# A hybrid recurrent decoder step on one core: loads moved to another DMA queue, two products made one, a sum taken from DMA to VectorE, and a new cut of the closing LayerNorm

## The chip, the cores and the metric

The kernel runs on one core of a Trainium2 chip. The metric is device time of one execution in microseconds; of the kernel before there are three runs, and their median counts. Engines are named as in the profile: PE is TensorE (PEld its weight loads), DVE is VectorE, ACT is ScalarE, POOL is GpSimd, SP is SyncE, which here only issues DMAs.

## The reference

One inference step of a single layer: a prompt of 512 tokens and 8 samples of one token each, which bring their states along. Everything is fp32.

```python
hq, hf, hi, hz, rq, rk, rv, rz, mq, mk, mv, mz, mo, mi, mf, gates = split(x @ w_in)   # 2048 -> 19464 columns
o_a = hgrn2(silu(hq), 1 - f, hi, f)           # 8 heads, 128 x 128;  f = lb + (1 - lb) * sigmoid(hf)
o_b = retention(rotary(rq), rotary(rk), rv)   # 4 heads, 256 x 256
h_c = mlstm(mq, mk, mv, mi, mf) * sigmoid(mo) # 4 heads, 256 x 256, with n and m beside C
ys  = head_norm(o) * silu(z)                  # for each of the three
out = sum_n(sigmoid(gates_n) * (ys_n @ w_branch[n])) @ w_out
y   = layernorm(alpha * x + out) * ln_g + ln_b
```

For a sample of retention, one step is `S = gamma * S + k v^T`, `o = q^T S`; for mLSTM the same with factors of its own, and a normaliser n.

## The kernel before

Tokens lie along the free axis: 512 of the prompt and 8 of the samples, `N` = 520 columns, in two halves of `HN` = 260. Each fp32 operand of a large product is cut into a high part, rounded to fp32r (`hi`, by ACT), and the rest (`lo`, by DVE); a product is then hi x hi, hi x lo and lo x hi on PE, in `PD` banks of PSUM.

The projection goes over 76 units of 256 columns of `w_in`. The first three are done plainly (`classical_w`). The other 73 use a Winograd form of Strassen's scheme (`strassen_unit`): seven items of 24 matmuls instead of eight, each on one block or sum of blocks of the weights. The blocks b11, b12 lie in one weight tile, b21, b22 in the next; tiles `R` come from a ring of three, 1 MB each. One of the sums, b11 + b12, lies in a tile of its own, `TT`. DVE makes it where the unit's columns are deinterleaved (`deint`) or where there is no unit before it; for the other units SP loads b11 into TT and an accumulating DMA of Pool's queue adds b12. The order of the units is: 16 for HGRN2, 16 for retention, 20 for mLSTM, 24 for the merge gates. Then come the branch products (`bunit`, 24 units of 256 columns of `w_branch`), the output projection (`ofin`), and LayerNorm.

`dense` writes out the items one after the other and yields after every few matmuls; at each yield `side_step` may add a step of three queues of side work: preparation, the scans of the heads (`a_head`, `b_head`, `c_head`), and the samples (`a_samp`, `bc_samp`). Whether it does is settled when the program is built, by a planner (`Clock`): it prices each instruction (in `Counted`), keeps a time for each engine and for DMA, and lets a step in when its time is due and DVE and ACT aren't further ahead than `clk.next` plus a margin. On the chip each engine just runs its instructions in the order written. A step whose data the planner holds for late (`late`) is put off.

Projected rows are stored to DRAM by Pool (`parked`, to `pk_...`) and loaded again by the head that needs them (`ld`) into slots `SL` of a pool of 16. `bc_samp(h, br)` handles the eight samples of one head in pairs: SP loads each state (`lds_`, 256 KB), Pool loads v (`ldv`), ACT scales v by the two halves of k into `tm` and `vb`, DVE updates the state's two halves, Pool stores it, and PE forms `o` by two products per sample, one for each half, whose weights are the query masked by sample (`qmask`, tile `qmt`: column b holds q of sample b, the others zeros); all go into the same PSUM rows `po` (`os` in the profile).

`norm_rows(c0)` normalises two blocks of 128 tokens: ACT scales a piece by the row's factor, DVE multiplies by `ln_g` (`lng`), DVE or Pool adds `ln_b` (`lnb`), SP stores. Blocks 0 and 1 come while PE works on the last half of the output, blocks 2 and 3 and the samples (`norm_samples`) after its end (`finish`).

Nearly all instructions are issued in the wrapper of `Counted`, line 165, and DMAs in its lines 142 and 143; so rows are told apart by the tiles that they write and read.

Of the kernel before, what the change touches and what calls it, by code (L numbers as in the profile page):

```python
# [17 lines left out]
D = 2048  # L18
# [100 lines left out]
class Counted:  # L119
# [3 lines left out]
    def __getattr__(self, op):  # L123
# [22 lines left out]
        def g(*a, **kw):  # L146
# [5 lines left out]
            if me == "pe":  # L152
                if op == "transpose":
                    t = 0.109 if out.shape[-1] > 64 else 0.06
                else:
                    n = a[2].shape[-1]
                    t = max(0.06, 0.00046 * n) if a[2].dtype == F32R else max(0.06, 0.00085 * n)
# [16 lines left out]
def tile_hybrid_step(  # L174
# [153 lines left out]
    qmt = const.tile([128, 2, 8, 8], F32, name="qmt")  # L328
# [97 lines left out]

    class Item:

        def __init__(self, src, mm, post=None, keep=None, nosplit=False):
# [3 lines left out]
            self.late = False  # L433
            self.part = None
# [65 lines left out]
    def strassen_unit(col, deint, fin):  # L500

        src = w_in[0][:, col:col + 256]
# [81 lines left out]
        if prev and not deint:  # L584
# [69 lines left out]
    def classical_rows(src, rws, xf, fin, pre=None):  # L654

        kt = 8 * rws
# [70 lines left out]
    def dense():  # L727
# [5 lines left out]
        for i, it in enumerate(items):  # L733
            it.run("first")
            clk.next = clk.pe + 2.87
# [46 lines left out]
    def ld(nm, k, pre=False):  # L782
        s = sl()
        SY.dma_start(out=v3(s[:, 0:S], 2), in_=d2(ptile(f"{nm}{k}"))[:, :, 0:256], pre=pre)
# [23 lines left out]
    def qmask(q, e):  # L808

        t = qmt[:, e]  # L810
        V.tensor_tensor(out=t, in0=e8, in1=q.unsqueeze(2).to_broadcast([128, NS, 8]), op=MUL)
        return t
# [208 lines left out]
    def a_samp(h):  # L1021
        q, K, f, z = sm("Aq", h), sm("AK", h), sm("Af", h), sm("Az", h)
        hb = {}
        qm = qmask(q, 0)
# [136 lines left out]
    def b_head(h):  # L1161
# [4 lines left out]
        for i in range(2):  # L1166
            SY.dma_start(out=cs2[i][:, 0:S], in_=rope[i, :, 0:S])
# [76 lines left out]
    def bc_samp(h, br):  # L1244
# [18 lines left out]
        def lds_(b):  # L1263
            st = yield from ssl()
            SY.dma_start(out=v3(st[:, 0:512], 2), in_=state_in[0, b, h].rearrange("(p t) v -> p t v", t=2), pre=True)
# [20 lines left out]
        qm = [qmask(q[e], e) for e in range(2)]  # L1286
        po = po1()
        for b0 in range(0, NS, 2):
# [6 lines left out]
            for bs in ([b0, b0 + 1],) if b0 + 1 in lds else ([b0], [b0 + 1]):  # L1295
# [24 lines left out]
                fr(tm)  # L1320
                yield 1
                for b in bs:
                    st = lds.pop(b)
                    for e in range(2):
                        T.matmul(po[0:NS, 0:256], qm[e][:, b, :], st[:, e * 256:(e + 1) * 256],
                                 start=(b == 0 and e == 0), stop=(b == 7 and e == 1))
                    fr(st)
                yield 1
# [249 lines left out]
    def w_unit(col, deint, fin):  # L1578
        strassen_unit(col, deint, fin)

# [36 lines left out]
    for i, (col, deint, fin) in enumerate(wl):  # L1617
# [4 lines left out]
        else:  # L1622
            strassen_unit(col, deint, fin)
# [143 lines left out]
    def norm_rows(c0):  # L1767
# [9 lines left out]
        for c in range(2):  # L1777
            hh = H[:, c0 + c, :]
            for q0, q1, e in (((0, 672, G), (672, 1344, G), (1344, 2048, V)) if c0 + c < 3 else
                              ((0, 640, G), (640, 1152, G), (1152, 1600, V), (1600, 2048, V))):  # L1780
# [326 lines left out]
```

## Time and profile before

| | |
|---|---|
| median of three runs | 2374.71 us (2374.15 to 2378.41) |
| the profiled execution: its time, its span | 2384.39 us, 2382.5 us |
| instructions in the span | 45461 |
| granted TensorE clock, mean | 0.992 |
| moved by DMA | 449.26 MB, 189 GB/s on average |
| on the queue of SP (hardware), of Pool (software) | 312.77 MB, 133.38 MB |

The time in the first row is what is forecast; all rows of the profile belong to the one profiled execution. Busy time is the time in which an engine worked on an instruction; matmuls are pipelined, so the mean of one is longer than the distance of two, and busy times of groups that overlap don't add up. A matmul of fp32 by fp32 leaves two records, one of fp32r leaves one. In the chain of waits each line has its start, its length, and the engine and tile or the DMA that it spent it on.

### The profile page before, as it was taken

The numbers are of one execution on the slowest core, as the hardware profiler recorded it, in microseconds if no ns is written. First come the engines' busy times: TensorE is split into PE (matmuls) and PEld (weight loads), VectorE is DVE, ScalarE is ACT, GpSimd is POOL, SyncE is SP. The second block draws the span as 40 slices with busy tenths as digits, with TensorE's granted clock in tenths as the row PEclk, the third lists the DMA queues.
The fourth block names the chain that finished last, engine by engine and source line by source line (L and its number), as shares of the span: only waits on it lengthen the run. The fifth ranks groups of instructions, "written<-read, shape, count | busy, mean of one in ns | idle before, by whom it ended". The sixth has DMA issues, their size and how long they took to land.

```text
span 2382.5 us, 45461 instructions
## 1 busy us (share of the span) xinstructions
PE 2318.9 (97%) x18677; PEld 2240.8 (94%) x18677; DVE 1603.2 (67%) x2571; ACT 1031.3 (43%) x1611; POOL 490.8 (21%) x653
## 2 busy tenths in 40 slices
PE   7999999999999999999999999999999999999995
PEld 7999999999999999999999899898999999999994
DVE  5777777787778868677777666767676534553336
ACT  4344445445545444454445545554554422222222
POOL 2022221323222132222122222212221100002002
PEclk9999999999999999999999999999999999999997
DMA  6367765647566576767767988889796767755221
GB/s 178 116 158 186 196 161 170 184 151 219 149 204 167 182 213 189 223 216 205 234 184 207 187 246 203 221 200 241 169 252 173 225 201 256 253 192 199 89 72 72
DMA packets 404690, 449.26 MB, mean 189 GB/s; under 512 B 16993, under 2 KB 356865, under 8 KB 402945
## 3 DMA queue, kind: packets, MB, share of 16 engines
q1 hardware_dynamic: 313664, 312.77, 42.3%
q0 software_dynamic: 90384, 133.38, 24.2%
q8 instruction: 147, 2.41, 0.4%
q14 instruction: 63, 0.51, 0.1%
q10 hardware_dynamic: 432, 0.20, 0.0%
HBM read 362.98 MB, written 83.28 MB: 187 GB/s over the span
## 4 chain that ended last, share of the span: by engine, by line
PE 61%; DMA 3%; DVE 1%; ACT 1%; issue 0%; POOL 0%; SPq 0%; DVEq 0%; POOLq 0%; ACTq 0%
PE PD L165 54%; PE s L165 4%; PE os L165 3%; DMA R<-in_w_in_dram 1%; DVE SL L165 1%; DMA out_dram<-SL 0%; DMA R<-in_w_branch_dram 0%; DMA TT<-in_w_in_dram 0%; ACT hi L165 0%; DVE lo L165 0%; ACT SL L165 0%; ACT TT L165 0%; DVE sdd L165 0%; DVE R L165 0%; DVE fmv L165 0%
## 5 line engine op out<-in xcount | busy, mean ns | idle before, releaser
L165 PE MATMUL PD<-XZ,hi 128*128 128x260 f32 x9920 | 1430.0, 285 | 13.3 <-ACT hi L165 10.0
L165 PEld LDWEIGHTS PD<-XZ,hi 128*128 128x128 f32 x9920 | 1282.7, 189 | 30.8 <-ACT hi L165 12.0
L165 DVE TENSOR_TENSOR lo<-R,hi 128x1024 fp32r<-128x1024 f32 (+1 forms) x540 | 646.1, 1198 | 381.2 <-ACT hi L165 161.6
L165 PE MATMUL PD<-XZ,lo 128*128 128x260 f32 x4944 | 799.4, 284 | 0.2 <-DVE lo L165 0.2
L165 ACT ACTIVATE hi<-R 128x1024 fp32r<-128x1024 f32 (+1 forms) x541 | 558.1, 1051 | 499.4 <-PE PD L165 254.8
L165 PEld LDWEIGHTS PD<-XZ,lo 128*128 128x128 f32 x4944 | 679.9, 189 | 5.5 <-issue 4.3
L165 ACT ACTIVATE SL<-PD 128x260 f32<-128x260 f32 x304 | 115.2, 381 | 424.3 <-PE PD L165 363.9
L165 POOL COPY smp<-SL 128x8 f32<-128x8 f32 x104 | 93.1, 895 | 535.3 <-ACT SL L165 344.2
L165 DVE TENSOR_TENSOR R<-R,R 128x1024 f32<-128x1024 f32 x146 | 178.0, 1219 | 6.4 <-DMA R<-in_w_in_dram 6.2
L165 DVE TENSOR_TENSOR SL<-SL 128x256 f32<-128x256 f32 (+9 forms) x315 | 146.4, 501 | 32.9 <-PE s L165 26.5
L165 PE MATMUL PD<-X,hi 128*128 128x260 f32 x1168 | 165.1, 287 | 0.3 <-ACT hi L165 0.3
L165 DVE TENSOR_TENSOR SL<-PD,SL 128x260 f32<-128x260 f32 x219 | 93.0, 425 | 99.4 <-PE PD L165 89.8
L165 PEld LDWEIGHTS PD<-X,hi 128*128 128x128 f32 x1168 | 148.4, 188 | 5.0 <-issue 4.1
L165 PE MATMUL s<-SL 128*128 128x64 f32 (+5 forms) x912 | 147.3, 298 | 0.0
L143 POOL DMA_DIRECT2D TT<-in_w_in_dram x56 | 90.2, 1610 | 272.7 <-DMA TT<-in_w_in_dram 245.5
L165 PEld LDWEIGHTS s<-SL 128*128 128x128 f32 (+1 forms) x912 | 125.0, 187 | 6.2
L165 ACT ACTIVATE SL<-SL 128x520 f32<-128x520 f32 (+5 forms) x156 | 85.2, 565 | 66.4 <-DVE SL L165 64.9
L142 POOL DMA_DIRECT2D out_dram<-SL x100 | 61.0, 614 | 217.9 <-DVE SL L165 196.3
L165 POOL TENSOR_TENSOR rstd<-rva,half 128x4 f32<-128x4 f32 (+3 forms) x35 | 45.2, 1292 | 247.5 <-DVE rva L165 247.4
L165 DVE TENSOR_TENSOR lo<-TT,hi 128x1024 fp32r<-128x1024 f32 x73 | 88.8, 1217 | 3.1 <-ACT hi L165 3.0
L165 DVE TENSOR_TENSOR R<-R 128x1024 f32<-128x1024 f32 x73 | 88.9, 1217 | 0.0
L165 PE MATMUL PD<-X,lo 128*128 128x260 f32 x584 | 84.7, 285 | 0.0
(213 smaller groups left out, 1416.7 us busy)
## 6 DMA issues: line engine op xcount, KB each, us to landing
R<-in_w_in_dram SPq DMA_DIRECT2D x150, 1024.0 KB, 6.3
TT<-in_w_in_dram SPq DMA_DIRECT2D x56, 512.0 KB, 6.4
TT<-in_w_in_dram POOLq DMA_DIRECT2D x56, 512.0 KB, 6.5
R<-in_w_branch_dram SPq DMA_DIRECT2D x24, 1024.0 KB, 6.5
out_dram<-SL POOLq DMA_DIRECT2D x88, 256.0 KB, 5.5
R<-in_w_out_dram SPq DMA_DIRECT2D x16, 1024.0 KB, 5.4
pk_g<-SL POOLq DMA_DIRECT2D x48, 260.0 KB, 4.7
SL<-pk_g SPq DMA_DIRECT2D x48, 260.0 KB, 5.9
```

The source lines that it names most:

```text
L142: return f(out=out, in_=in_)
L143: return f(out=out, in_=in_, accum_op=accum_op)
L165: return f(*a, **kw)
```

## The change

It has six parts.

1. `ld`, the rotary tables of `b_head` and the states of `bc_samp` are loaded on Pool's queue and no longer on SP's.
2. In `bc_samp` the two halves of a state are joined ahead of the product: ACT scales half 0 by the query, DVE adds half 1 times the query, and PE makes one product per sample with the constant mask `e8`. `qmask` remains for HGRN2 alone.
3. In `norm_rows` all additions are on DVE; there are eight equal pieces of 512 columns for each pair of blocks, and ACT scales a piece ahead.
4. For the last 24 units, the gates, `TT` is summed by DVE from the loaded tiles, as for a deinterleaved unit.
5. The planner prices a matmul of fp32 operands at twice as much.
6. The planner's look-ahead is 5.74 us for items of 48 matmuls and 2.87 us for items of 24, in place of 2.87 for all.

```diff
-                    t = max(0.06, 0.00046 * n) if a[2].dtype == F32R else max(0.06, 0.00085 * n)
+                    t = max(0.06, 0.00046 * n) if a[2].dtype == F32R else 2 * max(0.06, 0.00085 * n)
...
+    span = [5.74]
...
+            self.span = span[0]
...
-    def strassen_unit(col, deint, fin):
+    def strassen_unit(col, deint, fin, by_dma=True):
+        span[0] = 2.87
...
-        if prev and not deint:
+        if prev and not deint and by_dma:
...
     def classical_rows(src, rws, xf, fin, pre=None):
+        span[0] = 5.74
...
-            clk.next = clk.pe + 2.87
+            clk.next = clk.pe + it.span
...
     def ld(nm, k, pre=False):
-        SY.dma_start(out=v3(s[:, 0:S], 2), in_=d2(ptile(f"{nm}{k}"))[:, :, 0:256], pre=pre)
+        G.dma_start(out=v3(s[:, 0:S], 2), in_=d2(ptile(f"{nm}{k}"))[:, :, 0:256], pre=pre)
...
-            SY.dma_start(out=cs2[i][:, 0:S], in_=rope[i, :, 0:S])
+            G.dma_start(out=cs2[i][:, 0:S], in_=rope[i, :, 0:S])
...
         def lds_(b):
-            SY.dma_start(out=v3(st[:, 0:512], 2), in_=state_in[0, b, h].rearrange("(p t) v -> p t v", t=2), pre=True)
+            G.dma_start(out=v3(st[:, 0:512], 2), in_=state_in[0, b, h].rearrange("(p t) v -> p t v", t=2), pre=True)
...
-        qm = [qmask(q[e], e) for e in range(2)]
...
-                fr(tm)
                 yield 1
                 for b in bs:
-                    st = lds.pop(b)
-                    for e in range(2):
-                        T.matmul(po[0:NS, 0:256], qm[e][:, b, :], st[:, e * 256:(e + 1) * 256],
-                                 start=(b == 0 and e == 0), stop=(b == 7 and e == 1))
+                    i = (b % 2) * 256
+                    act(out=tm[:, i:i + 256], in_=lds[b][:, 0:256], func=AF.Copy, scale=q[0][:, b:b + 1])
+                yield 1
+                for b in bs:
+                    i, st = (b % 2) * 256, lds.pop(b)
+                    V.scalar_tensor_tensor(out=tm[:, i:i + 256], in0=st[:, 256:512], scalar=q[1][:, b:b + 1],
+                                           in1=tm[:, i:i + 256], op0=MUL, op1=ADD)
                     fr(st)
+                yield 1
+                for b in bs:
+                    i = (b % 2) * 256
+                    T.matmul(po[0:NS, 0:256], e8[:, b, :], tm[:, i:i + 256], start=(b == 0), stop=(b == 7))
+                fr(tm)
...
-            strassen_unit(col, deint, fin)
+            strassen_unit(col, deint, fin, i < len(wl) - 24)
...
-            for q0, q1, e in (((0, 672, G), (672, 1344, G), (1344, 2048, V)) if c0 + c < 3 else
-                              ((0, 640, G), (640, 1152, G), (1152, 1600, V), (1600, 2048, V))):
...
+        pieces = [(c, slice(q0, q0 + 512)) for c in range(2) for q0 in range(0, D, 512)]
...
+        scaled(*pieces[0])
+        for i, (c, qq) in enumerate(pieces):
+            if i + 1 < len(pieces):
+                scaled(*pieces[i + 1])
+            hh = H[:, c0 + c, qq]
+            V.tensor_tensor(out=hh, in0=hh, in1=g[:, qq], op=MUL)
+            V.tensor_tensor(out=hh, in0=hh, in1=b[:, qq], op=ADD)
+            SY.dma_start(out=y_p[0, (c0 + c) * 128:(c0 + c + 1) * 128, qq], in_=hh)
+            clk.latest = 0.0
+            yield 1
```

What this does to the order of instructions, at three places. First PE in the gates' stage, beside the samples of an mLSTM head, before. The products of the projection (`PD`) read `XZ` or `X` and a weight part; `os<-SL,qmt` are the samples' products, `s<-ident` transposes of a head.

```order
L165 MATMUL PD_127<-X_85,hi_121 128x260 x3
L165 MATMUL os<-SL,qmt 8x256 x4
L165 MATMUL PD_127<-X_85,hi_121 128x260 x13
L165 MATMUL PD_127<-X_85,lo_124 128x260 x8
L165 MATMUL PD_128<-XZ,hi_122 128x260 x3
```

The same in the changed kernel; `e_91` is the tile `e8`.

```order
L165 MATMUL s<-ident,SL 128x128 x4
L165 MATMUL PD_125<-XZ,hi_121 128x260 x3
L165 MATMUL os<-SL,e_91 8x256 x2
L165 MATMUL PD_125<-XZ,hi_121 128x260 x4
L165 MATMUL PD_125<-XZ,lo_124 128x260 x8
```

A pair of samples takes two products in place of four. In the whole program PE changes between fp32 products and the projection 656 times, both directions counted, where it was 642.

Second, SP's queue in the gates' stage, before. `R` are the ring of weights, `SL<-in_state_mlstm_c` the samples' states, `SL<-pk_...` loads by `ld`.

```order
L142 DMA SL<-in_state_mlstm_c_dram 128x512 x3
L142 DMA R_118<-in_w_in_dram 128x8x256
L142 DMA R_116<-in_w_in_dram 128x8x256
L142 DMA TT<-in_w_in_dram 128x8x128
L142 DMA R_117<-in_w_in_dram 128x8x256
L142 DMA SL<-in_state_mlstm_c_dram 128x512
L142 DMA R_118<-in_w_in_dram 128x8x256
L142 DMA TT<-in_w_in_dram 128x8x128
L142 DMA SL<-pk_mv_11769 128x2x256
```

SP's queue now, the last loads of the gates:

```order
L142 DMA R_118<-in_w_in_dram 128x8x256
L142 DMA R_116<-in_w_in_dram 128x8x256
L142 DMA R_117<-in_w_in_dram 128x8x256
L142 DMA R_118<-y_106 128x2048
L142 DMA R_116<-in_w_branch_dram 128x8x256
```

Only weights are left on it, one after the other, up to the first load of the branches (`y`). The other loads stand on Pool's queue, here at a place of the same stage, among the stores of gates (`pk_g`), of states (`out`), and the power for a norm (`rstd`):

```order
L142 DMA SL<-pk_mz_13703 128x2x256
L142 DMA out_dram<-SL 128x512
L142 DMA pk_g_10_17267<-SL 128x520
L142 DMA SL<-in_state_mlstm_c_dram 128x512
L142 DMA SL<-vs_111 128x512
L142 DMA SL<-in_state_mlstm_c_dram 128x512 x2
L142 DMA out_dram<-SL 128x512
L142 DMA pk_g_11_17388<-SL 128x520
L165 TENSOR_TENSOR rstd<-rva,half 128x4
```

Pool has 802 instructions where it had 658, SP 353 where it had 550.

Third, DVE at the end, from the last output tile to the norm of blocks 2 and 3: `SL<-SL,lng` multiplies, `SL<-SL,lnb` adds.

```order
-L165 TENSOR_TENSOR SL<-SL,lng 128x704
-L165 TENSOR_TENSOR SL<-SL,lnb 128x704
-L165 TENSOR_TENSOR SL<-SL,lng 128x672 x2
-L165 TENSOR_TENSOR SL<-SL,lng 128x704
-L165 TENSOR_TENSOR SL<-SL,lnb 128x704
+L165 TENSOR_TENSOR SL<-SL,lng 128x512
+L165 TENSOR_TENSOR SL<-SL,lnb 128x512
```

Where a multiplication and an addition alternated with multiplications whose additions Pool made, each multiplication is now followed by its addition; the two new rows are the first of five such pairs.

More of the change, by code (lines that the diff above doesn't have):

```diff
@@ L327, in tile_hybrid_step @@
     e8 = const.tile([128, 8, 8], F32, name="e8")
-    qmt = const.tile([128, 2, 8, 8], F32, name="qmt")
+    qmt = const.tile([128, 8, 8], F32, name="qmt")
     ones = const.tile([128, 1], F32, name="ones")
@@ L806, in put_ys, with qmask @@
         V.scalar_tensor_tensor(out=ysm[:, 8 * br + k, :], in0=psum, scalar=gains[:, br, k:k + 1], in1=z, op0=MUL, op1=MUL)
[L808 to L812, printed above, removed]
+    def qmask(q):
+        V.tensor_tensor(out=qmt, in0=e8, in1=q.unsqueeze(2).to_broadcast([128, NS, 8]), op=MUL)
+        return qmt
     def samp_silu(i0, n):
@@ L1023, in a_samp @@
         hb = {}
-        qm = qmask(q, 0)
+        qm = qmask(q)
         def get(b0):
@@ L1575, in c_head @@
         yield from room(0)
-    def w_unit(col, deint, fin):
-        strassen_unit(col, deint, fin)
     def plain(nm, k0):
@@ L1622, in tile_hybrid_step @@
         else:
-            strassen_unit(col, deint, fin)
+            strassen_unit(col, deint, fin, i < len(wl) - 24)
     first_strassen = 4 * NCL
@@ L1776, in norm_rows, with scaled @@
         yield 1
-        for c in range(2):
-            hh = H[:, c0 + c, :]
-            for q0, q1, e in (((0, 672, G), (672, 1344, G), (1344, 2048, V)) if c0 + c < 3 else
-                              ((0, 640, G), (640, 1152, G), (1152, 1600, V), (1600, 2048, V))):
-                qq = slice(q0, q1)
-                act(out=hh[:, qq], in_=hh[:, qq], func=AF.Identity, scale=r[:, c:c + 1], bias=nm[:, c:c + 1])
-                V.tensor_tensor(out=hh[:, qq], in0=hh[:, qq], in1=g[:, qq], op=MUL)
-                e.tensor_tensor(out=hh[:, qq], in0=hh[:, qq], in1=b[:, qq], op=ADD)
-                SY.dma_start(out=y_p[0, (c0 + c) * 128:(c0 + c + 1) * 128, qq], in_=hh[:, qq])
-                yield 2
+        pieces = [(c, slice(q0, q0 + 512)) for c in range(2) for q0 in range(0, D, 512)]
+        def scaled(c, qq):
+            hh = H[:, c0 + c, qq]
+            act(out=hh, in_=hh, func=AF.Identity, scale=r[:, c:c + 1], bias=nm[:, c:c + 1])
+        scaled(*pieces[0])
+        for i, (c, qq) in enumerate(pieces):
+            if i + 1 < len(pieces):
+                scaled(*pieces[i + 1])
+            hh = H[:, c0 + c, qq]
+            V.tensor_tensor(out=hh, in0=hh, in1=g[:, qq], op=MUL)
[3 more added lines that the diff above has]
+            yield 1
     def norm_samples():
```

## Prediction

> **What bounds the kernel now.** I read the busy shares first, then the same by stage, then the chain of work that ended last, then the waits of the engines that TensorE depends on. The busy shares (busy us, share of the span, instructions):
>
> ```profile
> PE 2318.9 (97%) x18677; PEld 2240.8 (94%) x18677; DVE 1603.2 (67%) x2571; ACT 1031.3 (43%) x1611; POOL 490.8 (21%) x653
> ```
>
> TensorE (PE) has work for 97% of the span, so time falls if PE has less to do or waits less, and hardly otherwise. The stages, with busy us of each engine, granted clock, DMA share and GB/s: 120 to 840 us are the HGRN2 projections, 840 to 1320 the retention heads beside the mLSTM projections, 1320 to 1800 the gates' projections beside the mLSTM heads, then branches, output projection, and the tail.
>
> ```profile
> 120.00:420.00 300.00, 296.86 (x2480) 295.38 (x2479) 230.25 (x344) 140.12 (x218) 69.45 (x82) 1.00 0.66 173
> 420.00:840.00 420.00, 417.16 (x3447) 405.74 (x3446) 331.79 (x571) 202.89 (x349) 117.65 (x153) 1.00 0.62 181
> 840.00:1320.00 480.00, 480.00 (x3752) 453.88 (x3751) 348.90 (x516) 230.32 (x344) 120.91 (x164) 1.00 0.72 206
> 1320.00:1800.00 480.00, 468.96 (x3606) 438.02 (x3606) 333.41 (x571) 245.64 (x386) 107.95 (x140) 0.99 0.88 215
> 1800.00:2180.00 380.00, 377.44 (x3149) 376.43 (x3148) 196.79 (x275) 115.85 (x142) 38.19 (x67) 1.00 0.67 220
> 2180.00:2340.00 160.00, 157.38 (x1300) 155.27 (x1298) 54.81 (x108) 35.38 (x53) 1.47 (x3) 1.00 0.27 86
> 2340.00:2382.50 42.50, 13.84 (x108) 13.25 (x107) 29.36 (x48) 11.82 (x16) 16.91 (x11) 0.68 0.26 101
> ```
>
> PE's idle time between 120 and 2340 us is 3.1 + 2.8 + 0 + 11.0 + 2.6 + 2.6 = 22.2 us. Half of it, 11.0, is in the gates' stage, where DMA is busiest (0.88); 28.7 more is the tail, in which PE has nearly done and DVE works. The clock is granted in full wherever PE is fed, so there is nothing to win there.
>
> **Samples' halves joined.** Of the chain, start and length of three pieces (records of TensorE), and the group of the samples' products:
>
> ```profile
> 1520.98 1.82 PE os L165 x8
> 1522.81 3.08 PE PD L165 x24
> ...
> 1886.12 289.55 PE PD L165 x2421
> ```
>
> ```profile
> L165 PE MATMUL os<-SL,qmt 128*8 128x256 f32 x256 | 61.9, 380 | 0.0
> ```
>
> For each sample and head of retention and mLSTM, PE multiplied two state halves with a masked query: 8 x 8 x 2 = 128 matmuls, which leave 256 records. On the chain 8 records cost 1.82 us, 0.2275 each, and the stream runs on without a gap. The change lets ACT scale one half by the query and DVE add the other, and PE does 64 matmuls with the constant e8: 128 records fewer, 29.1 us. The group's own 61.9 us (pipelined lengths, joined) would give 31.0, the other end. This lies on the engine that bounds, half of it in 840 to 1320 and half in 1320 to 1800. I take -29.1.
>
> What comes in instead, with the durations of like instructions (128x256 with a scalar per row on ACT and on DVE; the sum of two weight tiles on DVE):
>
> ```profile
> L165 ACT ACTIVATE SL<-SL,ks 128x256 f32<-128x256 f32 x128 | 62.2, 503 | 2.5 <-DMA SL<-vs 0.4
> L165 DVE SCALAR_TENSOR_TENSOR SL<-SL,scwb 128x256 f32<-128x256 f32 x64 | 27.6, 479 | 9.2 <-DMA SL<-in_state_mlstm_c_dram 6.0 <-ACT SL L165 3.0
> L165 DVE TENSOR_TENSOR TT<-R 128x1024 f32<-128x1024 f32 x17 | 20.7, 1218 | 6.2 <-DMA R<-in_w_in_dram 6.2
> ```
>
> ACT gets 64 x 0.503 = 32 us and DVE 64 x 0.479 = 31, half in each of the two stages. DVE also gets the 24 sums of the gates, 24 x 1.218 = 29 us, all in 1320 to 1800. ACT goes there from 246 to 262 of about 455 us and stays covered by PE. DVE goes from 333 to 333 + 15 + 29 = 378 of about 455, 83%. The row nearest to that is 420 to 840: DVE busy 332 of 420, 79%, and PE idle 2.8 of 420, 0.7%. So I put DVE's longer queue, behind which the low parts of the weights (lo) stand, at 0.7% of 455: +3. Its ends are 0, if its idle gaps take it all, and +10, the present idle time of this stage come again.
>
> **The gates' weights.** The chain, SP's queue, ACT's timeline, and the waits of PE (in this stage) and SP, one after the other:
>
> ```profile
> 1618.12 11.45 DMA out_dram<-SL
> 1630.01 6.43 DMA R<-in_w_in_dram
> ```
>
> ```profile
> 1623.41 6.55 SPq L142 DMA_DIRECT2D SL<-in_state_mlstm_c_dram  x2
> 1630.01 1.05 SPq L142 DMA_DIRECT2D R<-in_w_in_dram  x2
> ```
>
> ```profile
> 1636.47 2.01 ACT L165 ACTIVATE hi<-R 128x1024 fp32r<-128x1024 f32 x2 [3.25 <-DMA R<-in_w_in_dram]
> ```
>
> ```profile
> PE PD L165 <- ACT hi L165: 8.1, 4, 3.7
> ```
>
> ```profile
> SPq L142 <- DMA out_dram<-SL: 77.6, 17, 11.4
> ```
>
> Read in order: a sample's state load stands on SP's queue until a slot comes free, which takes a store of 11.45 us; two weight loads stand behind it and go out together at 1630.0; ACT idles 3.25 us for them, and PE waits for ACT's high part (hi). In this stage that wait is 8.1 us in four pieces. In the changed order the gates' weight loads follow each other on SP with no state load between them, since `ld` and the samples' loads are on Pool's queue. Beside that, 24 tiles are no longer fetched twice by DMA (512 KB each time, once plain and once accumulating): 25 MB less in a stage that moves 480 us x 215 GB/s = 103 MB. The loads there (KB, median us to landing):
>
> ```profile
> R<-in_w_in_dram SPq DMA_DIRECT2D x36, 1024.0 KB, 7.0
> TT<-in_w_in_dram POOLq DMA_DIRECT2D x19, 512.0 KB, 6.8
> ```
>
> With a quarter less traffic 7.0 should fall, so I take the 8.1 us as gone: -8. The ends are -11, the stage's whole idle time, and 0, if faster PE work uses up what the loads gain. What is late next there is DVE: the sum in TT and lo both wait for the same landing, 1.22 us one behind the other, inside the 1.95 us of PE's 16 products with hi (16 x 0.1196 by the long stretch of the chain above).
>
> **The loads moved to Pool.** 112 loads of heads and 64 of samples leave SP, 24 accumulating loads and 8 LayerNorm additions leave Pool. Rows of Pool's own issues:
>
> ```profile
> L143 POOL DMA_DIRECT2D TT<-in_w_in_dram x56 | 90.2, 1610 | 272.7 <-DMA TT<-in_w_in_dram 245.5 <-issue 16.5 <-DMA SL<-in_state_mlstm_c_dram 10.6
> L142 POOL DMA_DIRECT2D pk_g<-SL x48 | 26.6, 553 | 222.8 <-ACT SL L165 222.8
> ```
>
> Pool gains 176 x 0.553 = 97 us and loses 24 x 1.61 = 39 and some 14 of additions: 491 becomes about 535, 23% of the span, covered. Queued behind Pool's waits are now the loads as well: the accumulating load waits for its first half (245.5 us over the run) in the 32 units that keep it, and stores and the powers of the norms share the queue. Against this, a load no longer waits on SP for a ring buffer. I put the move by itself at 0; both signs are in the rivals.
>
> The issue price is the point that could be doubted: 48 issues took 0.553 us on average in a stage in which DVE was busy for 69%, so no issue was held up for long. The Trainium skill has a rule against this move (SBUF — State Buffer, "SBUF: two separate sides"): a DMA issued from Pool has its descriptors written by Pool's cores, and VectorE in a two-port mode locks them out, so the page advises SP or ACT. Its example, under "A bandwidth-pool intuition that's wrong", is about 620 ns alone against 3100 beside a copy; an estimate by that page would be 176 x 2.5 = 440 us more on Pool. By that rule the trace does not agree so far.
>
> **The planner and the tail.** Twice the price for an fp32 matmul and 5.74 us for the longer items move the side work, not its amount. The order changes between fp32 and projection products 656 times instead of 642, so it comes back to projections 7 times more. One return costs 3.08 - 24 x 0.1196 = 0.21 us: +1.5, with ends of 0 and 4.
>
> The tail's rows, in order of time, and DVE's like instruction of 512 columns:
>
> ```profile
> 2354.47 0.88 DVE L165 TENSOR_TENSOR SL<-SL,lng 128x704 f32<-128x704 f32 x1
> ...
> 2362.14 1.02 DVE L165 BATCH_NORM_AGGREGATE fmv<-AT 128x2 f32<-128x96 f32 x2
> ...
> 2364.25 0.16 DVE L165 SCALAR_TENSOR_TENSOR nm<-fmv,rstd 128x2 f32<-128x2 f32 x1 [0.89 <-POOL rstd L165]
> ...
> 2369.18 2.20 DVE L165 TENSOR_TENSOR SL<-SL,lng 128x704 f32<-128x704 f32 x1
> ...
> 2372.22 0.34 DVE L165 TENSOR_SCALAR trit<-trit,smu,rstd 128x128 f32<-128x128 f32 x1
> ...
> 2378.59 0.62 DVE L165 TENSOR_TENSOR SL<-SL,lnb 128x448 f32<-128x448 f32 x1
> ```
>
> ```profile
> L165 DVE TENSOR_TENSOR SL<-SL 128x512 f32<-128x512 f32 x88 | 58.2, 684 | 1.4 <-ACT SL L165 1.4
> ```
>
> A multiplication took 0.88 us while Pool was idle and 2.20 while Pool added. With all additions on DVE, five of the first eight pieces remain after PE's last product: 10 x 0.684 = 6.8 us in place of 2362.14 - 2354.47 = 7.7. The last eight take 1.0 to start (nm and ACT), 16 x 0.684 = 10.9, and 1.6 for eight small operations of the samples, the longest of them 0.34: 13.6 in place of 2379.2 - 2364.25 = 15.0. Together -2.2; the ends are 0 and -4.
>
> **Sum.** -29.1 + 3 - 8 + 0 + 1.5 - 2.2 = -34.8 us. The profiled execution took 2384.39 us (span 2382.5), 9.7 more than the median of the runs, 2374.71; every term is a difference, so I take it from the median: 2339.9, rounded 2340.
>
> **Rivals.** The saving is given back. PE is as early as its weights allow: near 1636 ACT waits for R before it can cut hi. If in the gates' stage the 14.6 us of saved products turn into waits, and the 11 us stay, it is 2374.7 - 14.6 - 2.2 + 1.5 = 2359. For it speaks that the loads take 7.0 us there; against it, that 25 MB leave, and that 840 to 1320 has no idle time at 0.72.
>
> The gain is larger. If the moved loads also clear the idle time of the other stages, up to 22.2 us in all, it is 2340 - 11 - 3 = 2326. For it speaks SP's 77.6 us of waits on stores over the whole run; against it, that the other 11.2 us are scattered.
>
> It becomes slower: loads late on Pool. There are some 68 groups of moved loads on which a head or a pair of samples starts (36 and 32), and PE's side products stand in order with the projections. If each group makes PE wait 0.51 us the gain is gone; from 0.58 on it is slower, and at 0.8 it is 2340 + 54 = 2394. For it speaks Pool's wait on the accumulating load; against it, that the planner asks for loads ahead and puts off a step whose data is late.
>
> The issue is locked out by DVE. If each group's first issue stood behind one 1.22 us instruction, and half of that reached PE, 68 x 0.61 = 41 us come back: 2381. The 0.553 us speak against it. The Trainium skill's page above would have it so.
>
> **How the numbers follow.** The forecast has 0.60, saving given back 0.19, larger gain 0.09, loads late 0.09, locked out 0.03. The likeliest case alone reaches from 2328 to 2350. The range goes up to the case of savings given back with the DVE term at its end, 2363, and down to the larger gain with the tail and the 31.0 at their ends, 2321. A difference under 0.2% (4.7 us) can't be told from none. Of late loads I count 0.03 there, of being locked out 0.01: faster 0.88, same 0.04, slower 0.08.
>
> **What would show it.** The os products of 256 columns should number 128 records at about 0.23 us on the chain. In the gates' stage PE's wait for hi should be under 3 us, DVE near 83%, SP with no wait on stores, the R loads under 7.0 us. Pool should be near 535 us with issues still near 0.55, and the tail about 2 us shorter. It is wrong if PE's waits for s and os products on loads (DMA SL) appear in many small pieces, if hi waits stay at 8 or more, or if lo becomes what PE waits for.

## The result: slower by 1.55%, and the profile after

Four runs of the changed kernel have a median of 2409.84 us (2408.23 to 2419.28), four of the kernel before beside them 2374.43: a ratio of 1.0155 (95% interval 1.0126 to 1.0184). The forecast was 2340, the range 2321 to 2363. The profiled execution took 2410.25 us, its span is 2408.5.

The busy shares of the changed kernel:

```profile
PE 2308.0 (96%) x18549; PEld 2240.4 (93%) x18549; DVE 1649.3 (68%) x2657; ACT 1058.7 (44%) x1678; POOL 538.6 (22%) x797
```

PE is busy for 10.9 us less than before and idle for 100.5 us instead of 63.6. The stages (busy us of PE, PEld, DVE, ACT, POOL, then clock, DMA share, GB/s):

```profile
420.00:840.00 420.00, 409.35 (x3342) 397.33 (x3342) 324.45 (x571) 199.49 (x346) 132.88 (x180) 1.00 0.60 173
840.00:1320.00 480.00, 468.87 (x3653) 448.03 (x3652) 354.11 (x530) 241.83 (x376) 154.83 (x229) 0.99 0.69 202
1320.00:1800.00 480.00, 451.74 (x3497) 430.19 (x3498) 358.88 (x587) 251.99 (x401) 111.76 (x182) 0.98 0.57 171
...
2340.00:2408.50 68.50, 40.94 (x328) 39.38 (x327) 38.60 (x82) 18.39 (x28) 2.27 (x3) 0.83 0.16 63
```

PE's idle time is now 10.7, 11.1 and 28.3 us in the three middle stages; it was 2.8, 0 and 11.0. DMA moves less in the gates' stage than before (171 GB/s for 215), and yet PE waits more. The waits of PE over the whole run (us in total, times, longest), the largest of the weights before, then now:

```profile
PE PD L165 <- ACT hi L165: 10.3, 7, 3.7
```

```profile
PE PD L165 <- ACT hi L165: 24.0, 20, 3.1
PE s L165 <- DMA SL<-pk_mo: 18.1, 7, 5.7
...
PE os L165 <- DVE SL L165: 7.5, 4, 3.0
```

Before, hi had 10.3 us in 7 waits and pk_mo none. All 18.1 us of pk_mo are in the gates' stage; hi has 4.3 there, 18.0 before it and 1.6 behind it. What the change was to do by itself happened: the samples' products have half the records, the new issues on Pool cost 0.54 to 0.85 us each, and Pool's busy time is 538.6 us, forecast 535:

```profile
L165 PE MATMUL os<-SL,e 128*8 128x256 f32 x128 | 33.8, 380 | 0.0
...
L142 POOL DMA_DIRECT2D SL<-in_state_mlstm_c_dram x32 | 17.3, 542 | 6.1 <-DMA out_dram<-SL 3.9 <-issue 1.2 <-PE os L165 1.0
...
L142 POOL DMA_DIRECT2D SL<-pk_rv x8 | 6.2, 846 | 0.0
```

### The profile page after: what moved, and what is told of

It reads as the page before. It is cut to its first block, busy times and chain, and to the rows that moved or that the text cites. A ratio compares the mean times of both kernels' runs of the same rounds, so it can differ in the third digit from the quotient of the medians.

```text
span 2408.5 us, 45112 instructions
## 1 busy us (share of the span) xinstructions
PE 2308.0 (96%) x18549; PEld 2240.4 (93%) x18549; DVE 1649.3 (68%) x2657; ACT 1058.7 (44%) x1678; POOL 538.6 (22%) x797
## 4 chain that ended last, share of the span: by engine, by line
PE 81%; DMA 10%; DVE 4%; issue 2%; ACT 2%; POOL 1%; SPq 0%; ACTq 0%; DVEq 0%; POOLq 0%
PE PD L165 71%; PE s L165 8%; DMA R<-in_w_in_dram 6%; PE os L165 2%; DMA SL<-pk_mo 2%; DVE SL L165 2%; DVE lo L165 1%; ACT hi L165 1%; DMA TT<-in_w_in_dram 1%; DVE R L165 1%; ACT SL L165 0%; DMA R<-in_w_branch_dram 0%; DVE XZ L165 0%; DMA nt<-in_state_mlstm_n_dram 0%; DMA SL<-in_x_prompt_dram 0%
## 5 line engine op out<-in xcount | busy, mean ns | idle before, releaser
L165 POOL COPY smp<-SL 128x8 f32<-128x8 f32 x104 | 87.2, 839 | 475.2 <-ACT SL L165 303.4
L165 DVE TENSOR_TENSOR SL<-SL 128x256 f32<-128x256 f32 (+8 forms) x315 | 146.4, 500 | 39.0 <-PE s L165 26.5
L165 ACT ACTIVATE SL<-SL 128x512 f32<-128x512 f32 (+5 forms) x156 | 85.8, 565 | 78.7 <-DVE SL L165 77.2
L165 PE MATMUL s<-ident,SL 128*128 128x128 f32 x389 | 64.0, 283 | 28.0 <-DMA SL<-pk_mo 18.1
L143 POOL DMA_DIRECT2D TT<-in_w_in_dram x32 | 52.0, 1624 | 160.6 <-DMA TT<-in_w_in_dram 125.3
```

The source lines that it names most:

```text
L143: return f(out=out, in_=in_, accum_op=accum_op)
L165: return f(*a, **kw)
```

## The experiments

All differences below are of medians, unless a ratio is named. The kernel before had medians of 2374 to 2381 us beside the different groups of runs, so a difference between groups is sure to some 5 us. Where the ratios to the kernel before give a difference that is over 5 us away from that of the medians, both are named. Every edit also changes what the planner reckons, and with it the order of the side work: in the traces PE's order is exactly that of the changed kernel only where the states alone, or mo and mz alone, went back to SP. The other differences hold some change of order too. The theories, as the expectations name them: Q, loads on Pool's queue and weights on SP's take the same DMA engines from each other; P, the planner's new prices; D, the gates' sums on DVE; N and S, something in Pool's queue itself; E, a few stores in very small pieces hold up all queues.

### Which part costs: the loads on Pool's queue

The moved loads back on SP, the rest as changed:

```diff
-        G.dma_start(out=v3(s[:, 0:S], 2), in_=d2(ptile(...))...)      # and rope, and the states
+        SY.dma_start(out=v3(s[:, 0:S], 2), in_=d2(ptile(...))...)
```

> The changed kernel with the heads', rotary and sample-state loads back on SP's queue; all else as changed. Changed: 2410 us, before: 2374. Theory Q (the moved loads now share the DMA engines with weight loads issued in the same microseconds, so both land late and TensorE waits): the pk_mo waits (18 us) and most of the hi waits outside the gates (about 17 us) go, and with them the slower clock behind each wait: 2345 to 2365. Theory P (the planner's new prices put side steps where their data isn't ready): no better than 2400. Theory D (the gates' sums on DVE): 2385 to 2395, since only the pk_mo wait goes.

Measured: 2367.11 us, ratio 0.9939 (0.9917 to 0.9962), 2 us above theory Q's range and far from the other two. The loads on Pool cost 43 us by the medians, 51 by the two ratios; without them the change makes the kernel faster. PE's busy time falls too, by 17.6 us: its clock stays up (0.993 for 0.987), which by estimate (2290.4 x 0.993 / 0.987) is worth 14 of them. The busy line, and PE's waits:

```profile
PE 2290.4 (97%) x18549; PEld 2227.4 (94%) x18549; DVE 1648.5 (70%) x2657; ACT 1058.5 (45%) x1678; POOL 434.3 (18%) x621
```

```profile
PE PD L165 <- ACT hi L165: 12.0, 7, 6.1
```

The same part alone, put into the kernel before (the diff reversed):

> The kernel before with one part of the change alone: ld, the rotary tables and the samples' states are loaded on Pool's queue. In the changed kernel this part cost 43 us (2410 against 2367). If that price is its own, this kernel takes 2379 + 43 = 2422. If it comes only where PE has less cover (joined halves, faster gates), it stays under 2395. If the 24 accumulating loads of the gates, which are still on Pool's queue here, stand behind the new loads, it goes over 2430, with waits of PE for hi in the gates above 25 us.

Measured: 2433.65, ratio 1.0226 (1.0203 to 1.0248), 56 us slower. So the price is the part's own. It is higher here, where the accumulating loads of the gates are on Pool's queue as well: 29.5 us of the waits for hi are in the gates' stage, as the third case of the expectation has it. Its waits of PE in the whole run:

```profile
PE PD L165 <- ACT hi L165: 38.3, 20, 12.7
...
PE s L165 <- DMA SL<-pk_mo: 9.1, 4, 3.5
```

Then the moved loads were split, in the changed kernel. First the states alone go back to SP, then `ld` and the rotary tables alone:

> The changed kernel with the samples' 64 states back on SP's queue; ld and the rotary tables stay on Pool's. Theory N: the states are asked for ahead and PE does not wait for them directly, so little comes back, 2398 to 2412, and PE's wait for pk_mo stays at 12 to 18 us. If the states were the price (Pool's queue full with 64 of the 176 loads), the time is under 2385.

> The changed kernel with ld and the rotary tables back on SP's queue; only the samples' 64 states stay on Pool's. With the states alone back on SP 7 us came back of 43. If the prices add, this gives back 36: 2374. If either group on Pool's queue is enough to make the weights late, it stays above 2385; if the states alone cost nothing, it is 2367.

Measured: 2403.74 and 2371.71. Of the 43 us, `ld` with the tables on Pool costs 37 and the states alone 5: the prices add within the spread, and the states, asked for ahead, cost little. Of the 37, 12 (19 by the ratios) are the 16 loads of mo and mz:

```diff
-        G.dma_start(out=v3(s[:, 0:S], 2), ...)
+        (SY if nm in ("mo", "mz") else G).dma_start(out=v3(s[:, 0:S], 2), ...)
```

> The changed kernel, with 16 of the 176 moved loads, those of mo and mz, back on SP's queue. Theory N: they land in 5 to 7 us as they did there, PE's wait for pk_mo goes, and with it 18 us and the slow clock behind it: 2380 to 2392, waits for hi unchanged at about 24 us. Theory Q (loads and weights take each other's bandwidth): the wait for pk_mo goes, but weights land later, waits for hi grow by 10 or more, 2395 to 2410.

Measured: 2397.47. The waits for pk_mo are gone, mo lands after 6.8 us in place of 10.1, but PE's waits for hi grow from 24.0 to 29.3. The time is in theory Q's range; the waits for hi grow as it says, but by half of its 10.

### Why the weights come late

A place of the changed kernel that shows it. At 845.6 us SP issues two weight loads and at 851.7 the first half of a TT; from 850.3 to 854.2 Pool issues six loads for a retention head. The issues from 844 to 856 us (KB, median us to landing), in the changed kernel and with the loads on SP:

```profile
R<-in_w_in_dram SPq DMA_DIRECT2D x2, 1024.0 KB, 9.9
SL<-c_rope_dram POOLq DMA_DIRECT2D x2, 256.0 KB, 6.7
SL<-pk_rq POOLq DMA_DIRECT2D x2, 256.0 KB, 7.3
TT<-in_w_in_dram SPq DMA_DIRECT2D x1, 512.0 KB, 12.9
```

```profile
R<-in_w_in_dram SPq DMA_DIRECT2D x1, 1024.0 KB, 8.2
TT<-in_w_in_dram SPq DMA_DIRECT2D x1, 512.0 KB, 7.7
SL<-c_rope_dram SPq DMA_DIRECT2D x2, 256.0 KB, 7.9
```

On SP the head's loads stood behind TT, which came first. On Pool they pass it: the loads of rq, issued at 851.4 with TT, land some 5 us ahead of it, and TT takes 12.9 us for 7.7. In these 12 us Pool's queue moved 1.91 MB and SP's 1.87. The Trainium skill (DMA: Bandwidth & Descriptors, "Queues, rings and completion order") says that a DMA engine goes round the queues that have work for it, packet by packet. By that a second queue takes a share and isn't put behind the first, and these rows agree. How that reaches PE stands in the chain of waits (start, length, what):

```profile
848.08 13.98 DMA R<-in_w_in_dram
...
864.38 1.23 DVE R L165
...
869.48 1.14 DVE lo L165
...
870.63 9.85 DMA R<-in_w_in_dram
...
880.56 1.06 ACT hi L165
...
881.67 18.44 PE PD L165 x139
```

A weight load in flight for 14 us makes DVE late; DVE gives the ring's buffer back late, so the next load goes out late (870.63), with two states just ahead of it on Pool's queue, and lands late. At 881.67 PE has stood for 3.11 us. With the loads on SP, PE has 0.1 us of idle time in the whole of 840 to 1320 (columns as in the stages):

```profile
840.00:1320.00 480.00, 479.92 (x3787) 460.37 (x3786) 368.54 (x555) 251.29 (x393) 124.59 (x168) 1.00 0.71 209
```

The moved loads were not tried on a third queue, ACT's. So it is not shown what of the price any second queue would cost, and what is due to Pool's queue in particular.

Is it bandwidth? Half of each moved load, without the stores of n that are told of below:

```diff
-        G.dma_start(out=v3(s[:, 0:S], 2), in_=d2(ptile(...))[:, :, 0:256], pre=pre)
+        G.dma_start(out=v3(s[0:64, 0:S], 2), in_=d2(ptile(...))[0:64, :, 0:256], pre=pre)   # rope and states alike
```

> The changed kernel without the stores of n (left out, as in the run before that took 2391) and with half of each moved load: only 64 of 128 partitions of the parked rows, rotary tables and states are fetched, on Pool's queue, the other half of the slots holds what was there. It leaves 24 us to explain against 2367 with whole loads on SP. Theory Q (what is left is that the loads take the DMA engines from the weights): the weight loads of 840 to 1320 us land earlier, PE's waits for hi fall from 26 to 16 or less, the time to 2372 to 2382. If what is left is not bandwidth but the queue itself, its order or Pool's issues, the time stays at 2387 to 2393.

Measured: 2382.76, 8 us less than with whole loads (2390.96), just outside the range of Q, with hi at 20.3 us instead of 26.1 (Q had 16 or less). At the place above, with a different order of issues, the landings in this run are:

```profile
R<-in_w_in_dram SPq DMA_DIRECT2D x1, 1024.0 KB, 5.3
...
SL<-pk_rq POOLq DMA_DIRECT2D x2, 128.0 KB, 5.2
```

So half of the bytes went along with 8 us. But in 840 to 1320 PE's idle time did not fall (467.5 us busy for 470.1), since other stalls came, one of 4.29 us at 989. The planner prices a DMA by its bytes as well and gave another order. So it is likely, but not shown, that bytes are part of the price; how it divides into bytes, order and chance meetings of transfers is left open.

### Stores in small pieces

The largest waits are those for pk_mo. The issues of Pool from 1430 to 1445 us:

```profile
SL<-pk_mo POOLq DMA_DIRECT2D x2, 256.0 KB, 9.5
...
out_dram<-SL POOLq DMA_DIRECT2D x1, 1.0 KB, 7.9
```

The store of 1 KB is the mLSTM's n, one column of a tile: 256 pieces of 4 bytes. Stretches of 3 us there (columns as in the stages):

```profile
1433.00:1436.00 3.00, 3.00 (x27) 3.00 (x26) 2.32 (x3) 2.98 (x5) 2.65 (x5) 1.00 0.38 126
1436.00:1439.00 3.00, 3.00 (x26) 2.86 (x24) 3.00 (x5) 1.71 (x3) 1.82 (x3) 1.00 1.46 51
1439.00:1442.00 3.00, 0.07 (x1) 0.00 (x0) 2.62 (x3) 0.87 (x3) 0.09 (x1) 1.00 0.69 27
1442.00:1445.00 3.00, 0.74 (x3) 0.45 (x3) 0.00 (x0) 0.71 (x1) 0.00 (x0) 0.61 0.76 269
1445.00:1448.00 3.00, 3.00 (x15) 3.00 (x15) 1.40 (x4) 0.00 (x0) 0.00 (x0) 0.50 0.26 96
```

For 6 us the DMA engines count as busy (1.46 and 0.69 of their time, packets that overlap counted each) and move 51 and 27 GB/s; then mo lands and PE goes on, after 4.75 us, at half its clock (0.50). The kernel before has such stretches too, and one of them is the very place from which the prediction read the gates' 8 us. There Pool issued a store of n at 1609.9 us, and the rate stayed low from 1615 to 1624:

```profile
1612.00:1615.00 3.00, 3.00 (x27) 3.00 (x26) 2.76 (x4) 0.87 (x3) 1.61 (x1) 1.00 1.26 316
1615.00:1618.00 3.00, 3.00 (x27) 2.96 (x25) 2.82 (x4) 1.84 (x4) 0.00 (x0) 1.00 1.09 24
1618.00:1621.00 3.00, 3.00 (x22) 2.22 (x21) 2.36 (x2) 2.42 (x5) 2.18 (x4) 1.00 1.36 27
1621.00:1624.00 3.00, 3.00 (x27) 3.00 (x27) 1.90 (x5) 0.62 (x1) 0.00 (x0) 1.00 0.62 28
```

The state's store of 11.45 us in the prediction's chain, for which SP's queue stood, was issued at 1618.12, inside this stretch; the median of the 256 KB stores in that stage is 5.5 us. The order of SP's queue put the weights behind that store, but what made the store late is, by these rows, the store of n.

To test it in the changed kernel, the store was first put on another queue:

```diff
-        G.dma_start(out=mn_p[0, 0, h].rearrange("(p t) -> p t", t=2), in_=n2[:, :, 256])
+        A.dma_start(out=mn_p[0, 0, h].rearrange("(p t) -> p t", t=2), in_=n2[:, :, 256])
```

> The changed kernel, with one store of c_head, that of n (256 pieces of 4 bytes, 1 KB, four times in the run), issued on ACT's queue instead of Pool's. In the trace it stands right ahead of the loads of mo and mz and lands after 7.8 us, they after 10.1 and 10.8. Theory N (one queue: the loads stand behind Pool's own stores, this one above all): the mo loads land in under 7.5 us, PE's wait of 18.1 us for pk_mo falls under 6, and the time is 2380 to 2392. Theory Q (what is shared are the DMA engines): the pieces pass the same engines from another queue, mo still lands in about 10 us, and the time is 2405 to 2415.

Measured: 2417.64, ratio 1.015 (1.0123 to 1.0176), a little above theory Q's range. PE's wait for pk_mo falls to 11.4 us, not under 6, and that for hi grows to 38.6. The landings stay:

```profile
SL<-pk_mo POOLq DMA_DIRECT2D x8, 256.0 KB, 11.2
...
out_dram<-SL ACTq DMA_DIRECT2D x4, 1.0 KB, 9.1
```

Theory N falls: the loads do not stand behind the store in a queue. Next the stores of n were left out, `mn_p` (four times) and the samples' `mn_s` (four times 8 KB, in 1024 pieces of 8 bytes, not the 2048 that the expectation names):

> The changed kernel without the mLSTM's stores of n (left out: four of 1 KB in 256 pieces of 4 bytes, four of 8 KB in 2048 pieces; their outputs are not written). In the trace no byte of a load moves for some 3 us after one of them, and all that is issued beside it lands late, weights on SP's queue too (14.7 us in the kernel before). Theory E (the pieces hold up the DMA engines for every queue): loads of mo land in under 8 us, PE's 18 us of waits for pk_mo fall under 6, the time is 2380 to 2395. Theory S (loads on Pool's software queue are late by themselves): mo stays at 9 us or more and the time at 2402 to 2412.

Measured: 2390.96, ratio 1.0045 (1.003 to 1.006): 19 us less (26 by the ratios), as theory E says. The waits for pk_mo are gone, those for hi are not (26.1 us). The landings of mo, over the whole run:

```profile
SL<-pk_mo POOLq DMA_DIRECT2D x8, 256.0 KB, 3.9
```

Do they hold up the weights of SP's queue too? The same with the loads on SP, under both planners:

> The fastest version so far (2361: loads on SP, old planner, joined halves, gates' sums on DVE) without the mLSTM's stores of n (left out). Beside the loads on Pool those stores cost 19 us. If they hold up the engines for all queues, PE's waits for hi of about 3.9 us at 1507 and 1655 us, each some 12 us or less after such a store, go here too and the time is 2350 to 2357. If only loads on Pool's queue suffer from them, it stays at 2359 to 2364.

> The changed kernel with the moved loads on SP and without the mLSTM's stores of n (left out); the new planner stays. It is the fourth corner of loads (Pool or SP) and stores of n (with or without): 2410, 2367, 2391 so far. If the stores of n cost the same 18 to 19 us whichever queue the loads are on, it takes 2346 to 2352, and the price of the loads on Pool's queue is 42 us with them and without. If part of that price is only that loads on Pool's queue suffer from the stores, it takes 2358 to 2367 and the price is 24 to 33 without them.

Measured: 2343.56 with the old planner (2361.38 with the stores), less than the 2350 to 2357 expected, and 2357.18 with the new one (2367.11 with them). The stores cost 18 and 10 us with all loads on SP: they hold up the weights of SP's queue too. So the kernel before most likely paid for them as well; it was not run without them. In the old planner's run PE's waits for hi fall from 13.3 us to

```profile
PE PD L165 <- ACT hi L165: 1.5, 3, 0.7
```

By the four corners of one planner (2409.84, 2367.11, 2390.96, 2357.18) the loads on Pool cost 43 us with the stores and 34 without, so 9 are the meeting of the two, nearly as the second case of the expectation has it. By the ratios it is 51 and 32: so it is likely that the two meet, but by how much is not sure.

### The gates' sums

In the changed kernel the accumulating DMA again, first with the loads on Pool, then on SP; and the sums on DVE alone, put into the kernel before:

```diff
-            strassen_unit(col, deint, fin, i < len(wl) - 24)
+            strassen_unit(col, deint, fin)
```

> The changed kernel with the gates' sums by accumulating DMA again; all else as changed. Theory Q: the gates' stage gets its 25 MB of traffic back and the pk_mo loads land later still: 2410 to 2425. Theory P: about 2410. Theory D: DVE waits less for weights (12 us of waits of the sum in the gates' stage go): 2385 to 2400.

> The changed kernel with the moved loads back on SP and the gates' sums by the accumulating DMA again; with three versions measured (both parts as changed 2410, loads on SP 2367, gates by DMA 2454) it is the fourth corner. If the 44 us that the gates' sums on DVE were worth beside the loads on Pool are their own, it takes 2367 + 44 = 2411. If they are worth that only where accumulating loads and moved loads share Pool's queue, and about the 8 us of the prediction otherwise, it takes 2372 to 2380.

> The kernel before with one part alone: the gates' sums on DVE instead of the accumulating DMA. The prediction gave it 8 us, less 3 for DVE's longer queue: 2369 to 2374 against 2377. If it is worth tens of microseconds by itself, as beside the loads on Pool, it is under 2350. If PE merely waits for lo instead, it is 2377 or more.

Measured: 2454.25 with the loads on Pool, ratio 1.0305 (1.0282 to 1.0329); 2371.22 with the loads on SP, ratio 0.9965 (0.995 to 0.9981); 2380.72 for the sums on DVE alone, ratio 1.0001 (0.9989 to 1.0013). Theory D falls, DVE's sums do no harm; but no theory had a number near the first, and theory Q's 2410 to 2425 was the nearest. The sums on DVE save 44 us (36 by the ratios) beside loads on Pool, 4 with the loads on SP, and nothing alone. In the first run, 24 accumulating loads share Pool's queue with the moved ones, and PE waits

```profile
PE PD L165 <- ACT hi L165: 65.2, 26, 7.8
```

In the run with this part alone the gates' stage did improve, by 5.1 us (PE busy 474.1 of 480 for 469.0), yet no time is left of it.

### Joined halves alone, and the planner

The kernel before with the joined halves alone (part 2 of the change):

> The kernel before with nothing but the samples' halves joined (64 fewer fp32 matmuls on TensorE, 64 more scalings on ACT and as many additions on DVE). If the products' 29 us on TensorE are saved whole: 2346. If side work was filling time in which weights were on their way, part comes back as waits for hi: 2355 to 2370. If DVE and ACT get late by it: 2375 or more.

Measured: 2372.43, ratio 0.9975 (0.9963 to 0.9986), 6 us. The busy line and the first new wait:

```profile
PE 2291.8 (97%) x18549; PEld 2229.5 (94%) x18549; DVE 1626.0 (69%) x2619; ACT 1057.6 (45%) x1675; POOL 477.2 (20%) x653
```

```profile
PE s L165 <- DMA SL<-pk_mo: 10.5, 3, 9.1
PE PD L165 <- ACT hi L165: 10.1, 9, 3.8
```

PE's busy time falls by 27.1 us, forecast 29.1; its idle time rises by 14.3, of which 10.5 are waits for pk_mo, on SP's queue here. (By these figures the profiled execution is 12.8 us shorter than that of before, which took longer than its median; by the medians 6 are left.) The longest of the waits comes behind a store of n, issued at 1774.6 us (so do the three longest of the changed kernel, of 4.5, 4.8 and 5.7 us):

```profile
1788.00:1791.00 3.00, 0.00 (x0) 0.00 (x0) 0.00 (x0) 0.00 (x0) 0.00 (x0) 0.50 0.64 53
```

```profile
1792.19 0.47 PE L165 MATMUL s<-ident,SL 128*128 128x128 f32 x1 [9.05 <-DMA SL<-pk_mo]
```

So the faster stream meets a load that is late, and the largest part of that lateness comes beside a store of n. The joined halves without these stores were not run alone.

The planner's old price and look-ahead, in the changed kernel, and in the one with the loads on SP:

```diff
-                    t = ... else 2 * max(0.06, 0.00085 * n)
+                    t = ... else max(0.06, 0.00085 * n)
...
-            clk.next = clk.pe + it.span
+            clk.next = clk.pe + 2.87
```

> The changed kernel with the planner's old price for fp32 matmuls and the old look-ahead of 2.87 us; all else as changed. Theory Q: 2395 to 2415, the loads are still on Pool's queue. Theory P: 2345 to 2365. Theory D: 2400 to 2415.

> The changed kernel with the moved loads back on SP and with the planner's old price and old look-ahead; what is left of the change are joined halves, the gates' sums on DVE and the LayerNorm tail. With the loads on SP but the new planner, PE had 8.8 us of idle time in 420 to 840 us where the kernel before had 2.8, in four waits for hi of 1.5 to 2 us. If the new prices cause them (theory P), they go and the time is 2358 to 2363; if not, it stays at 2365 to 2370.

Measured: 2408.01, by the medians 2 us under 2409.84 (10 by the ratios, whose intervals overlap), so theory P falls; and 2361.38, ratio 0.9918 (0.9901 to 0.9936), 6 us better than 2367.11. There PE is busy for 417.1 us of 420 to 840, as before, and not for 411.2. The waits for hi of that stage, five with 5.0 us in all and none over 1.6 (the expectation has four of 1.5 to 2), are down to one of 0.4: they were the planner's. Without the stores of n the new planner costs more, 14 us (2357.18 against 2343.56).

### A version that beats both

The loads on SP, the old planner, joined halves, the gates' sums on DVE, the LayerNorm pieces, and n written in rows: TensorE transposes it, DVE interleaves it into a row.

```diff
-        G.dma_start(out=mn_p[0, 0, h].rearrange("(p t) -> p t", t=2), in_=n2[:, :, 256])
+        pn = ps()
+        for e in range(2):
+            T.transpose(pn[0:1, e * 128:(e + 1) * 128], n2[:, e, 256:257], ident)
+        w = sl()
+        V.tensor_copy(w[0:1, 0:256].rearrange("b (p t) -> b t p", t=2), pn[0:1, 0:256].rearrange("b (t p) -> b t p", t=2))
+        G.dma_start(out=mn_p[0, 0, h].unsqueeze(0), in_=w[0:1, 0:256])
+        fr(w)
...                                          # mn_s alike, eight rows; second run: after a yield 2
```

> The same version with the stores of n kept, but written in rows: TensorE transposes n, DVE copies it into a row, and the store has one piece of 1 KB (prompt) or eight of 1 KB (samples) instead of 256 or 1024 or more small ones. If the number of pieces is the price, it comes within 3 us of the run without those stores, 2351 to 2359; if the store as such holds things up, or the added 16 transposes and 8 copies, it stays at 2361 or above.

> The fastest full version so far (2358: loads on SP, old planner, n written in rows), with the samples' transposes of n put two steps of side work later. There PE waited for nt four times, 1.1 to 2.0 us, 5.4 in all, and once 3.7 us for hi. If those waits are the price of the rows, they fall under 1 us and the time to 2350 to 2355; if the store itself or DVE's copies cost, it stays at 2357 to 2361.

Measured: 2358.15, inside the expected range, but only 3 us under the version with small pieces (2361.38) and 15 above that without the stores; then 2348.36, ratio 0.9874 (0.9858 to 0.9891), below the expected 2350 to 2355. Landings of the rows and the wait of PE in the first of the two; then the wait for hi in the second, where that for nt is gone:

```profile
out_dram<-SL POOLq DMA_DIRECT2D x4, 8.0 KB, 3.3
out_dram<-SL POOLq DMA_DIRECT2D x4, 1.0 KB, 1.7
```

```profile
PE os L165 <- DVE nt L165: 5.4, 4, 2.0
```

```profile
PE PD L165 <- ACT hi L165: 3.1, 4, 1.5
```

The same bytes land in 3.3 and 1.7 us in place of 8.5 and 8.3, so the cutting into small pieces was the price; whether by the number of pieces or by their size (4 and 8 bytes; as rows 64 bytes and 1 KB) is not told apart. The rows with their 16 transposes and 8 copies keep 5 of the 18 us, and moving the samples' part two steps later was worth 10.

## Why the prediction was wrong, step by step

**Loads moved to Pool: 0 was taken, some 43 us were measured.** This is the step that failed. The prediction put the move by itself at nothing: it priced the issues, which came out as said (Pool 538.6 us), and asked whether the loads would be late for the heads. It did not ask whom they would make late. As the place at 845 us shows, on SP a load stood behind the weights that were issued ahead of it, and that order was a priority; on a second queue it shares the engines with them. The rival "loads late on Pool" had the sign, a chance of 0.09 and 2394 us, but only one of the victims, the heads: against the run with the loads on SP, PE is idle for 31 us more, of which pk_mo has 18.1 and hi 12, and busy for 17.6 us more with the same work, for the most part by its lower clock (0.987 for 0.993). The sign that the text named, waits for DMA SL in pieces, did appear, but for pk_mo alone; they went with the stores of n, and also with mo and mz back on SP. (One reading of that step is off, without weight in the sum: the 245.5 us of Pool's waits belong to all 56 accumulating loads, and the 32 that stay had 125.3.)

**Joined halves: -29.1 was taken, about -6 measured alone.** PE's work fell by 27.1 us, so the price per record was right. That the stream would run on without a gap was not: half came back as idle time, three waits for pk_mo above all. The rival "saving given back" had this mechanism, but named the weights, not a parked row, as what is late next. With the loads on SP, the old planner and no stores of n, joined halves, the gates' sums and the tail come to 37 us under the kernel before (2343.56 against 2381.03 beside it), so more of the saving may be there once those stores are out of the way; which part has how much of it is not shown.

**The gates' weights: -8 was taken, 0 to -4 measured where the loads are on SP.** In the changed kernel's gates' stage R lands in 6.0 us (forecast: under 7.0), SP waits no longer for stores ahead of a load, and PE's wait for hi falls from 8.1 to 4.3 (forecast: under 3). So the step did about half of what was said, and pk_mo, with 18.1 us in this very stage, took its place. The 0 to -4 are the price of the sums alone; the other half of the step, no state loads ahead of the weights, can't be had without the moved loads. Alone the sums left no gain in the time, though the stage had 5.1 us less idle time; why is open. The prediction also took what it saw at 1618 us for the order of SP's queue alone and did not ask why a store took 11.45 us; leaving out the stores of n, one of which stood beside it, saved 10 to 19 us, more than these sums. (In its working, 16 x 0.1196 is 1.91, not 1.95; nothing hangs on it.)

**DVE's longer queue: +3.** DVE's share in the gates' stage was 75%, not 83; the sums on DVE alone cost nothing that can be measured. PE's waits for lo, which it was to make longer, are 1.3 us in the whole run.

**The planner: +1.5, ends 0 and 4; measured +6 with the loads on SP, +14 there without the stores of n, and +2, within the spread, on Pool.** It was priced by changes of mode on PE. What it did was something else: in 420 to 840 us it let side work in at other times, and with the loads on SP PE waited five times for hi, 5.0 us in all. Why it costs more without the stores of n is open.

**The tail: -2.2 was taken, -2.3 measured.** From the end of PE's last products of 128 columns (2353.74 us before, 2382.04 after) to the end of the span it was 28.8 us and is 26.5. The pieces came as forecast, too: DVE's five pairs ahead of the aggregation took 6.6 us (6.8), and from `nm` to the last addition it took 13.4 (13.6).

**Locked out by DVE.** This rival fell: issues on Pool took 0.54 to 0.85 us, DVE being 68% busy. The Trainium skill (SBUF — State Buffer, "A bandwidth-pool intuition that's wrong") gives its 3100 ns for a whole DMA beside a copy on DVE, not for the issue on Pool; no new issue here comes near that. Whether DVE's instructions here lock Pool out as that copy does, no run shows.

**The sum.** The forecast was 34.8 us down, the measurement 35.4 up, 70 apart. With the loads taken last, 43 of the 70 are the loads, some 23 the joined halves and some 4 the gates' sums; the planner's 4 or so and the 3 of DVE's queue, which did not come, cancel within the spread.

## What to carry to other kernels

Before you move transfers from one queue to another, ask what they stood behind there: here one queue was an order, two queues were a division, and the stream that bounds the kernel paid for it. When a transfer in a trace takes twice its usual time, ask what else was in flight beside it before you blame the queue's order. Price a saving on the bounding engine by what is late next, over all that it waits for and not only the weights. When two parts of a change touch one resource, measure the corners: the gates' sums were worth 0, 4 or 44 us, by where the loads were.

## What the runs showed of the hardware

A store of 1 KB in 256 pieces of 4 bytes took 7.8 us to land in the changed kernel and 12.8 in the kernel before (medians of four). Beside it all DMA together moved 27 to 51 GB/s for 6 us in the one and 24 to 28 for 9 us in the other. As a row, in 16 pieces of 64 bytes, it took 1.7 and 4.8 us (medians of the two runs with rows). The eight stores of n, 36 KB in all, cost 10 to 19 us of some 2370 by the medians, in three pairs of runs.

After PE had waited for 4.75 us its granted clock was 0.50 (1445 to 1448 us):

```profile
1443.82 0.47 PE L165 MATMUL s<-ident,SL 128*128 128x128 f32 x1 [4.75 <-DMA SL<-pk_mo]
...
1444.86 3.17 PE L165 MATMUL PD<-XZ,hi 128*128 128x260 f32 x13
1447.82 1.88 PE L165 MATMUL PD<-XZ,lo 128*128 128x260 f32 x8
```

From 1444.86 to 1449.70 these are 21 products in 4.84 us; at the prediction's 0.1196 us each they take 2.51. So by estimate this wait cost some 2.3 us more than itself. The Trainium skill (TensorE: Matmul & The Clock Gate, "What's actually happening") has half the clock after an idle window of about 3.4 us; the rows agree.
